# Retention woven into the attention in small steps, modulation sums by column groups, and a down projection that turns its tiles later

## The chip, the cores and the metric

One core of a Trainium2 chip. The metric is the device time of one execution in microseconds (us). TensorE (PE) multiplies a stationary 128-row tile with a moving one, VectorE (DVE), ScalarE (ACT) and GpSimd (POOL) work elementwise, SyncE (SP) issues most DMAs. Each engine runs its instructions in program order.

## The reference

Two layers of a trunk of width 1024 over 9 tiles of 128 tokens: 8 latent tiles and one context tile (`CTX` = 8). All in float32.

```
each layer:  h = rmsnorm(x) * g1 * (1 + scale) + shift        # modulation: six rows of 1024 per layer,
             q,k,v.. = h @ w_in                                #   silu(c) @ w_ada + b_ada, for c and c_ctx
             A = retention(q, k, v)     B = Fourier mixing
             C = latent attention       D = long convolution   # 4 x 256 columns
             x = x + gate * rmsnorm([A B C D] @ w_out) * g2
             x = x + gate * rmsnorm(swiglu(h2) @ w_down) * g4

retention, per head (4 of 64), forward and backward over chunks of 128 tokens:
   S[j+1] = gamma^128 * S[j] + (k * zeta)^T v
   o[j]   = (q k^T * D) v  +  (q * xi) S[j]
```

The final retention states of the context are an output too.

## The kernel before

The layers run one after the other, each in stages: input projection with convolution ("phase 1"), Fourier, retention and attention ("phase 2"), output projection ("phase 3"), the gate and up products of the FFN (`gate_up`, a Strassen scheme, 22 hidden blocks), and the down projection (`ffn`). The source lists instructions with priorities; a scheduler turns them into one fixed order per engine, with semaphores between engines.

**Modulation** (`ada_steps`, from L254). The two conditioning rows are multiplied with the 6144 columns of `wada` in groups of 256 columns: eight loads `adw` of 128x256 (L263); for row 0 VectorE adds each, scaled, into `adacc0` (L160, called by L267); for row 1 ScalarE scales it into `adp` (L272) and GpSimd adds (L157). TensorE then sums over the 128 partitions, with the 128x2 selector `sel` as the stationary tile: two products with `adacc0` and `adacc1` into `psada`, 2x256 (L285). VectorE adds the bias (`r`, in an `adw` buffer, loaded by L280) and multiplies by the norm's gain (`ng`, in an `adp` buffer, L282), and a DMA stores the row (L290). `adw` and `adp` have two buffers, `adacc` one. The function is a generator, advanced between products: the last 16 groups of layer 0 run in its phase 1 (there VectorE does both rows), the 24 of layer 1 in layer 0's `gate_up`, five advances for each group.

**Retention** (`ret_rope`, `ret_tables`, `ret_states`, `ret_tile`, `ret_group`). `ret_states` makes the nine (k * zeta)^T v (`pskv`, L1062), copies their diagonal blocks into `Sall` (L1071) and runs the recurrence on VectorE. All of that stands ahead of the attention, with a higher priority. `ret_tile` then makes one tile: four turns (L1088), four score products on 64 rows (L1100), the decay (L1101), and for each head one product with `v` (L1107) and two with the states, of 64 rows and 64 columns (L1110).

**Attention** (`attention`, L946). 20 items (a head and a pair of tiles) in a pipeline: scores of item n (L129 to L131, each product as three of split operands), turns of n - 1 (L918, L923), values of n - 2 (L935, L936, L938, result `o` L942). After the values it calls `beside(n)`, which advances the retention by one tile or group: 20 calls, 12 of them with work.

**Down projection** (`ffn`, from L1469). Three groups of three tiles; the products `dq` of a group go over 22 hidden blocks, in seven runs per tile. After the last run of a tile `finish` follows: norm of the product, `y` (L160), `x + y` (L157, on GpSimd for tiles up to `ET`, which is tile 7 in layer 0 and 1 in layer 1), then in layer 0 the norm and modulation of the next layer (L313, and the shift on the same engine as `x + y`), and at once eight turns (`norm_turn`, L324) whose results are the next layer's input.

Of the kernel before, what the change touches and what calls it, by code (L numbers as in the profile page):

```python
# [99 lines left out]
class Kern:  # L100
# [137 lines left out]
    def load_cond(self):  # L238
# [6 lines left out]
        self.sel = self.cp.tile([P, 2, 2], F32, name="sel")  # L245
        nc.vector.memset(self.sel, 0.0)
        for i in range(2):
            nc.vector.memset(self.sel[:, i, i:i + 1], 1.0)
# [5 lines left out]
    def ada_steps(self, l, c0, n, pool, psp, tag, dve=(0, 1)):  # L254


        nc, A = self.nc, self.A
        for c in range(c0, 6 * D, n):
            s, hs = c // D, slice(c % D, c % D + n)
            acc = [pool.tile([P, n], F32, name=f"adacc{i}", bufs=1) for i in range(2)]  # L260
            for kt in range(8):
                w = pool.tile([P, n], F32, name="adw", bufs=2)
                nc.sync.dma_start(w, A["wada"][l, kt, :, c:c + n])  # L263
                for i in range(2):
                    cs = self.cs[:, kt, i:i + 1]
                    if i in dve and kt:
                        self.stt(acc[i], w, cs, acc[i], ALU.mult, ALU.add)  # L267
                    elif i in dve:
                        self.ts("v", acc[i], w, cs)
                    else:  # L270
                        d = acc[i] if kt == 0 else pool.tile([P, n], F32, name="adp", bufs=2)
# [6 lines left out]
            k = {1: 0, 2: 1, 4: 2, 5: 3}.get(s)  # L278
            r, ng = (pool.tile([P, n], F32, name=nm, bufs=2)[:2] for nm in ("adw", "adw" if len(dve) > 1 else "adp"))
            nc.sync.dma_start(r, A["bada"][l, s:s + 1, hs].broadcast_to([2, n]))  # L280
            if k is not None:
                nc.sync.dma_start(ng, A["normg"][l, k:k + 1, hs].broadcast_to([2, n]))  # L282
            ps = psp.tile([2, n], F32, name="psada", tag=tag)
            for i in range(2):
                nc.tensor.matmul(ps, self.sel[:, i], acc[i], start=i == 0, stop=i == 1)  # L285
            nc.vector.tensor_tensor(out=r, in0=ps, in1=r, op=ALU.add)
            if k is not None:
                nc.vector.scalar_tensor_tensor(out=r, in0=r, scalar=1.0 if s in (1, 4) else 0.0, in1=ng,
                                               op0=ALU.add, op1=ALU.mult)
            nc.sync.dma_start(self.mods[l, s][:, hs], r)  # L290
            yield
# [654 lines left out]
    def attention(self, l, pool, hd, psp, beside):  # L946
# [6 lines left out]
        for n in range(len(pairs) + 2):  # L953
# [24 lines left out]
    def ret_tables(self, l, pool, Sall):  # L978
# [33 lines left out]
        scratch = Sall[:, 4:8].rearrange("p t a b c -> p (t a b c)").rearrange("p (n c) -> p n c", c=P)  # L1012
# [15 lines left out]
    def ret_rope(self, l, keep):  # L1028
# [4 lines left out]
        Sall = keep.tile([P, 8, 2, 2, 64], F32, name="Sall")  # L1033
        self.qk = keep.tile([P, NT, 512], F32, name="rqk")
        for t in range(NT):
            if t % 3 == 0:
                nc.sync.dma_start(self.qk[:, t:t + 3], self.proj[l][:, t:t + 3, 256:768])
            if t < CTX:
                tmp = Sall[:, 2 * (t % 2):2 * (t % 2) + 2].rearrange("p a b c d -> p (a b c) d")
# [3 lines left out]
    def ret_states(self, l, zt, gt, Sall, keep, psp):  # L1043

        nc, A = self.nc, self.A
        kvc = keep.tile([P, 2, 2, 64], F32, name="kvc")
        kzs = keep.tile([P, 2, 2, 4, 64], F32, name="rkz", tag="ropeR")
        for d in range(2):
            nc.sync.dma_start(Sall[:, 7 * d, :, d], A["sret"][l, :, :, d])
        for t in range(NT):  # L1050
            if t % 3 == 0:
                v3 = keep.tile([P, 3, 256], F32, name="rv")
# [11 lines left out]
            for hh in range(2):  # L1064
# [4 lines left out]
                for d, dst in ((0, t + 1), (1, t - 1)):  # L1069
                    if 0 <= dst < 8:  # L1070
                        nc.scalar.activation(Sall[q, dst, :, d], ps[q, :, d, q], AF.Copy)  # L1071

        nc.sync.dma_start(A["o_st"][l], kvc)
        for d, order in ((0, range(1, 8)), (1, range(6, -1, -1))):
            for t in order:
                prev = t - 1 if d == 0 else t + 1
                tmp = keep.tile([P, 2, 64], F32, name="rst")
                self.tt("v", tmp, Sall[:, prev, :, d], gt[:, :, d:d + 1].broadcast_to([P, 2, 64]), ALU.mult)
                self.tt("v", Sall[:, t, :, d], Sall[:, t, :, d], tmp, ALU.add)

    def ret_tile(self, l, t, vg, o, Dm, xi, Sall, pool, psp):
# [7 lines left out]
        qkT = pool.tile([P, 4, P], F32, name="rqkT")  # L1089
        nc.scalar.activation(qkT, ps, AF.Copy)  # L1090
        if lat:
            qx = pool.tile([P, 2, 2, P], F32, name="rqx")
            self.tt("g", qx, qkT[:, 0:2].unsqueeze(2).broadcast_to([P, 2, 2, P]), xi, ALU.mult)

# [7 lines left out]
        for e in range(2):  # L1102
            q = slice(64 * e, 64 * e + 64)
            pi = psp.tile([P, 2, 64], F32, name="psr", tag="r")
            for pr in range(2):
                h = 2 * pr + e
                nc.tensor.matmul(pi[:, pr], sT[:, h], vg[:, 64 * h:64 * h + 64], start=True, stop=not lat)  # L1107
                if lat:
                    for d in range(2):
                        nc.tensor.matmul(pi[:, pr], qx[q, pr, d], Sall[q, t, pr, d], start=False, stop=d == 1)  # L1110
            nc.scalar.activation(o[:, e::2], pi, AF.Copy)

    def ret_group(self, l, g, Dm, xi, Sall, pool, psp):

        nc = self.nc
        vg = pool.tile([P, 3, 512], F32, name="rvg")
        o = pool.tile([P, 12, 64], F32, name="ro", bufs=1)
        for j in range(3):
            self.ret_tile(l, 3 * g + j, vg[:, j], o[:, 4 * j:4 * j + 4], Dm, xi, Sall, pool, psp)
            yield  # L1120
# [19 lines left out]
        for j in range(3):  # L1140
# [3 lines left out]
            rt = pool.tile([P, 2, P], F32, name="rot", bufs=4)  # L1144
# [61 lines left out]
    def phase2(self, l):  # L1206
        nc, tc, A = self.nc, self.tc, self.A
        with ExitStack() as c:
# [478 lines left out]
```

## Time and profile before

| | us |
|---|---|
| median of 3 runs | 3466.37 (3465.84 to 3473.54) |
| the profiled execution | 3473.78 |
| its span | 3472.0 |
| PE busy | 3195.8 (92%) |
| DVE busy | 2421.7 (70%) |
| ACT busy | 1269.0 (37%) |
| POOL busy | 704.6 (20%) |

The stages, read from the timeline by their lines: layer 0 has phase 1 up to 560 us, phase 2 up to 848, phase 3 up to 965, `gate_up` up to 1537 and the down projection up to 1850; in layer 1 they end at 2240, 2551, 2660, 3178 and 3472. A busy PE is not a PE at full speed: PEclk is the share of its full clock that it was granted.

### The profile page before, as it was taken

The page shows a single profiled execution, that of the slowest core. Times are in us where ns is not written, and L with a number is a line of the kernel's source. Part 1 is how long each engine was busy: PE and PEld are TensorE (multiplying, and loading weights), DVE is VectorE, ACT ScalarE, POOL GpSimd, SP SyncE. Part 2 cuts the span into 40 slices and gives each one's busy share as a digit, 9 for nine tenths or more (in the row PEclk, how much of TensorE's full clock was granted, in tenths as well). Part 3 has the DMA queues.
Part 4 walks back from the last instruction along what each step waited for, and adds up shares of the span by engine and source line. Part 5 has one row for each costly group of instructions (what it writes and reads, how often), then busy time and mean ns, then how long its engine had stood idle before and what let it go on. Part 6 is the DMA issues. An engine that isn't in the chain of part 4 may idle for free.

```text
span 3472.0 us, 52651 instructions
## 1 busy us (share of the span) xinstructions
PE 3195.8 (92%) x19198; PEld 2844.6 (82%) x19198; DVE 2421.7 (70%) x4806; ACT 1269.0 (37%) x2384; POOL 704.6 (20%) x625
## 2 busy tenths in 40 slices
PE   8889888999969999989988999899997999998998
PEld 5768777888769999977777788798886899998887
DVE  6676887767898888874456637676688866665454
ACT  3123213555344444443333232254544322223332
POOL 2101110001244545521111011100112422220000
PEclk8799999889989999999999999998898999999999
DMA  5354555114333434364554444541053322225564
GB/s 213 102 173 141 156 166 179 39 38 138 104 124 118 124 114 123 103 204 163 174 170 138 136 125 142 172 125 34 23 172 110 94 77 77 77 65 172 173 206 142
DMA packets 343827, 444.64 MB, mean 128 GB/s; under 512 B 63338, under 2 KB 273511, under 8 KB 343056
## 3 DMA queue, kind: packets, MB, share of 16 engines
q1 hardware_dynamic: 281792, 384.31, 35.5%
q10 hardware_dynamic: 61776, 56.97, 5.4%
q8 instruction: 151, 2.47, 0.3%
q14 instruction: 108, 0.88, 0.1%
HBM read 349.17 MB, written 92.00 MB: 127 GB/s over the span
## 4 chain that ended last, share of the span: by engine, by line
PE 56%; DVE 21%; DMA 10%; issue 5%; ACT 4%; POOL 3%; SPq 0%; DVEq 0%; ACTq 0%; POOLq 0%
DMA adw<-in_wada 7%; PE gu L129 5%; PE gu L131 5%; PE gu L130 5%; PE dq L129 4%; PE dq L131 4%; PE dq L130 4%; DVE adacc L160 3%; PE acc L131 3%; PE acc L130 2%; PE acc L129 2%; PE pstr L918 1%; PE psr L1110 1%; DVE rq_w L146 1%; DVE fw L125 1%
## 5 line engine op out<-in xcount | busy, mean ns | idle before, releaser
L129 PE MATMUL dq<-dw 128*128 128x512 f32 x792 | 312.4, 394 | 13.5 <-ACT dw L120 10.8
L130 PE MATMUL dq<-dw 128*128 128x512 f32 x792 | 312.4, 394 | 0.0
L131 PE MATMUL dq<-dw 128*128 128x512 f32 x792 | 311.3, 394 | 0.0
L129 PE MATMUL gu<-X,fw 128*128 128x256 f32 x1024 | 286.8, 283 | 7.7 <-ACT fw L120 4.2
L160 DVE SCALAR_TENSOR_TENSOR adacc<-adw,csilu,adacc 128x256 f32<-128x256 f32 x392 | 228.5, 609 | 86.2 <-DMA adw<-in_wada 84.8
L131 PE MATMUL gu<-X,fw 128*128 128x256 f32 x1024 | 284.3, 280 | 1.9 <-DVE fw L125 1.9
L130 PE MATMUL gu<-X,fw 128*128 128x256 f32 x1024 | 283.8, 280 | 0.0
L130 PE MATMUL acc<-wlo,Th 128*128 128x256 f32 (+1 forms) x720 | 214.0, 297 | 6.6 <-DVE wlo L125 6.6
L125 DVE TENSOR_TENSOR dw<-dhr,dw 128x384 fp32r<-128x384 f32 x132 | 74.4, 569 | 208.5 <-ACT dw L120 207.2
L129 PE MATMUL acc<-whi,Th 128*128 128x256 f32 (+1 forms) x720 | 215.8, 302 | 0.8 <-ACT whi L120 0.4
L131 PE MATMUL acc<-whi,Tl 128*128 128x256 f32 (+1 forms) x720 | 214.5, 298 | 0.0
L129 PEld LDWEIGHTS gu<-X,fw 128*128 128x128 f32 x1024 | 193.7, 190 | 18.6 <-ACT fw L120 7.0
L131 PEld LDWEIGHTS gu<-X,fw 128*128 128x128 f32 x1024 | 193.6, 190 | 2.3 <-DVE fw L125 2.3
L130 PEld LDWEIGHTS gu<-X,fw 128*128 128x128 f32 x1024 | 193.7, 190 | 0.0
L129 PEld LDWEIGHTS dq<-dw 128*128 128x128 f32 x792 | 151.1, 191 | 47.1 <-ACT dw L120 11.9
L157 POOL TENSOR_TENSOR adacc<-adacc,adp 128x256 f32<-128x256 f32 x168 | 151.8, 903 | 160.7 <-ACT adp L272 157.1
L125 DVE TENSOR_TENSOR dw<-dwr,dw 128x1024 fp32r<-128x1024 f32 x132 | 161.4, 1225 | 31.3 <-ACT dw L120 31.2
L129 PE MATMUL gu<-x1s,fw 128*128 128x320 f32 x576 | 179.3, 311 | 3.7 <-DVE u L157 3.1
L131 PE MATMUL gu<-x1s,fw 128*128 128x320 f32 x576 | 179.4, 312 | 1.9 <-DVE fw L125 1.7
L130 PE MATMUL gu<-x1s,fw 128*128 128x320 f32 x576 | 179.0, 311 | 0.0
L131 PEld LDWEIGHTS dq<-dw 128*128 128x128 f32 x792 | 151.0, 191 | 32.5 <-DVE dw L125 1.3
L130 PEld LDWEIGHTS dq<-dw 128*128 128x128 f32 x792 | 151.2, 191 | 31.2
(494 smaller groups left out, 9432.5 us busy)
## 6 DMA issues: line engine op xcount, KB each, us to landing
dwr<-in_wf SPq DMA_DIRECT2D x132, 512.0 KB
adw<-in_wada SPq DMA_DIRECT2D x320, 128.0 KB
dhr<-h SPq DMA_DIRECT2D x132, 192.0 KB
h<-U SPq DMA_DIRECT2D x176, 128.0 KB
X<-in_wf SPq DMA_DIRECT2D x42, 512.0 KB
fr<-in_wf SPq DMA_DIRECT2D x40, 512.0 KB
pj<-pst ACTq DMA_DIRECT2D x90, 128.0 KB
r<-mod SPq DMA_DIRECT2D x20, 512.0 KB
```

Of the source, the lines that this page charges most:

```text
L125: (nc.vector if elo == "dve" else nc.gpsimd).tensor_tensor(out=lo, in0=src, in1=hi, op=ALU.subtract)
L129: mm(ps, lh, rh, start=start, stop=False)
L130: mm(ps, lh, rl, start=False, stop=False)
L131: mm(ps, ll, rh, start=False, stop=stop)
L146: nc.vector.scalar_tensor_tensor(out=w, in0=a, scalar=a[:, 0:1], in1=v, op0=ALU.mult, op1=ALU.mult)
L157: (self.nc.vector if e == "v" else self.nc.gpsimd).tensor_tensor(out=out, in0=a, in1=b, op=op)
L160: self.nc.vector.scalar_tensor_tensor(out=out, in0=a, scalar=s, in1=b, op0=op0, op1=op1)
L918: T(pst[:, j], pr[i][:, (k0 + j) * P:(k0 + j + 1) * P], self.ident)
L1110: nc.tensor.matmul(pi[:, pr], qx[q, pr, d], Sall[q, t, pr, d], start=False, stop=d == 1)
```

## The change

1. **Sums of the modulation.** Per group, four products instead of two: 32 stationary columns of ones, 128 moving columns, each into its own 32 partitions of a 128x128 `psada`. Bias, gain and result move in two DMAs each. In `gate_up` the sum stands three advances later (`late=3`), `adacc` has two buffers, `adp` one (which `ng` shares), and a group takes four advances instead of five.
2. **Retention.** `ret_states` and a tile's three parts are advances of their own: 11 for the states, 27 for tiles, 6 for groups, 44 together. `beside(n)` is also called after each scores: 64 calls. A state in `Sall` is 128 columns wide with zeros off the diagonal, so the product with the states takes 128 rows and columns, four for a tile instead of eight, and one copy `ro` instead of two.
3. **Down projection.** `x + y` and the shift are VectorE's for all tiles. The turns wait in a list `late`; one entry is taken after the first run of the next group's first tile, or when there are two.

```diff
+        def total(c, acc):
...
+            r, ng = (pool.tile([P, n], F32, name=nm, bufs=1 if late and nm == "adp" else 2)[:, :m]
+                     for nm in ("adw", "adw" if len(dve) > 1 else "adp"))
...
+            for h in range(2):
+                for i in range(2):
+                    q = 64 * h + 32 * i
+                    nc.tensor.matmul(ps[q:q + 32], self.ones[:, 0:32], acc[i][:, m * h:m * h + m], start=True, stop=True,
+                                     tile_position=(0, q))
...
-            acc = [pool.tile([P, n], F32, name=f"adacc{i}", bufs=1) for i in range(2)]
+            acc = [pool.tile([P, n], F32, name=f"adacc{i}", bufs=2 if late else 1) for i in range(2)]
...
+                    step += 1
+                    if todo and todo[0][0] <= step:
+                        total(*todo.pop(0)[1:])
                     yield
+            step += 1
+            todo.append((step + late, c, acc))
+            if not late:
+                yield
+                total(*todo.pop(0)[1:])
             yield
...
                 if i < len(score):
                     probs[n].append(self.att_scores(score[i], ops[h], pool, psp))
+                beside(n)
...
-        Sall = keep.tile([P, 8, 2, 2, 64], F32, name="Sall")
+        Sall = keep.tile([P, 8, 2, 2, P], F32, name="Sall")
...
+        pi = psp.tile([P, 4, 64], F32, name="psr", tag="r")
+        for pr in range(2):
+            both = pi[:, 2 * pr:2 * pr + 2].rearrange("p h e -> p (h e)")
+            if lat:
+                nc.tensor.matmul(both, qx[:, pr, 0], Sall[:, t, pr, 0], start=True, stop=False)
+            for h in (2 * pr, 2 * pr + 1):
+                nc.tensor.matmul(pi[:, h], sT[:, h], vg[:, 64 * h:64 * h + 64], start=not lat, stop=not lat)
+            if lat:
+                nc.tensor.matmul(both, qx[:, pr, 1], Sall[:, t, pr, 1], start=False, stop=True)
+        nc.scalar.activation(o, pi, AF.Copy)
+        yield
...
-                zt, gt, Dm, xi = self.ret_tables(l, rk, Sall)
-                self.ret_states(l, zt, gt, Sall, rk, psp)
+                tabs = self.ret_tables(l, rk, Sall)
...
+            steps = self.retention(l, tabs, Sall, rk, rp, psp)
...
-                ada = self.ada_steps(1, 0, 256, adp, banks, "ad", (0,))
+                ada = self.ada_steps(1, 0, 256, adp, banks, "ad", (0,), 3)
...
-                    self.tt(e, x[:, q], x[:, q], y[:, q], ALU.add)
+                    self.tt("v", x[:, q], x[:, q], y[:, q], ALU.add)
...
-                    self.norm_mod(t, x, y, rows[1], rows[2], dn, "tr", None, e)
+                    self.norm_mod(t, x, y, rows[1], rows[2], None, None, None, "v")
+                    late.append((t, y))
...
+                        if len(late) > 1 or late and f0 == 3:
+                            self.norm_turn(*late.pop(0), dn, "tr")
                         if f0 + n == NF:
                             finish(3 * g + j, ps[j])
```

What the scheduler makes of it, at three places. First TensorE's order in the attention of layer 0, around one retention tile. Before (`sc` scores, `pstr` turns, `psr` the retention's products, `psr<-Sall` those with the states):

```order
L918 MATMUL pstr<-ident,pr 128x128 x4
L1100 MATMUL psr<-rqkT 128x128 x4
L918 MATMUL pstr<-ident,pr 128x128 x2
L1107 MATMUL psr<-rvg,rsT 128x64
L1110 MATMUL psr<-Sall,rqx 128x64 x2
L1107 MATMUL psr<-rvg,rsT 128x64
L1110 MATMUL psr<-Sall,rqx 128x64 x2
L918 MATMUL pstr<-ident,pr 128x128 x3
```

And after the change:

```order
L131 MATMUL sc<-at_Tl_5835,at_Th_5834 128x384
L1142 MATMUL psr<-Sall,rqx 128x128
L1144 MATMUL psr<-rvg,rsT 128x64 x2
L1146 MATMUL psr<-Sall,rqx 128x128
L1142 MATMUL psr<-Sall,rqx 128x128
L1144 MATMUL psr<-rvg,rsT 128x64 x2
L1146 MATMUL psr<-Sall,rqx 128x128
L937 MATMUL pstr<-ident,pr 128x128 x8
```

A tile's products with the states are four instead of eight, and scores stand between them and the tile's turns and scores, which have moved to other items.

Second TensorE's order in `gate_up` of layer 0, around one sum of the modulation (`gu` are the products of the stage). Before:

```order
L130 MATMUL gu<-x1s_9234,fw 128x320
L131 MATMUL gu<-x1s_9233,fw 128x320
L285 MATMUL psada<-adacc_12001,sel 2x256
L285 MATMUL psada<-adacc_12002,sel 2x256
L129 MATMUL gu<-X_8153,fw 128x256
L130 MATMUL gu<-X_8154,fw 128x256
```

After:

```order
L129 MATMUL gu<-x1a_9249,fw 128x320
L272 MATMUL psada<-adacc_11481,ones 32x128
L130 MATMUL gu<-x1a_9250,fw 128x320
L272 MATMUL psada<-adacc_11482,ones 32x128
L272 MATMUL psada<-adacc_11481,ones 32x128
L272 MATMUL psada<-adacc_11482,ones 32x128
L131 MATMUL gu<-x1a_9249,fw 128x320
```

A sum is four products, here split by one of the stage's own. Counted over the whole stage in units of one hidden block (168 products `gu`), the 24 sums stand from 2.86 to 22.0, 0.83 apart, before, and from 3.29 to 20.32, 0.74 apart, after.

Third VectorE's order at the end of tile 0 of layer 0's down projection (the small operations between are those of the square root). Before:

```order
L160 SCALAR_TENSOR_TENSOR y_16753<-dq,rs,r_16537 128x1024
L303 TENSOR_SCALAR ss<-ss 128x1
...
L125 TENSOR_TENSOR dw<-dhr,dw 128x384
L313 SCALAR_TENSOR_TENSOR y_16753<-x_16543,rs,r_16539 128x1024
L150 SCALAR_TENSOR_TENSOR rq_u<-rq_w,rs 128x1
L125 TENSOR_TENSOR dw<-dwr,dw 128x1024
```

After:

```order
L160 SCALAR_TENSOR_TENSOR y_16877<-dq,rs,r_16661 128x1024
L157 TENSOR_TENSOR x_16667<-x_16667,y_16877 128x1024
L322 TENSOR_SCALAR ss<-ss 128x1
...
L125 TENSOR_TENSOR dw<-dhr,dw 128x384
L332 SCALAR_TENSOR_TENSOR y_16877<-x_16667,rs,r_16663 128x1024
L150 SCALAR_TENSOR_TENSOR rq_u<-rq_w,rs 128x1
L125 TENSOR_TENSOR dw<-dwr,dw 128x1024
L157 TENSOR_TENSOR y_16877<-y_16877,r_16665 128x1024
```

Both adds are now VectorE's. In TensorE's order the turns of the three tiles of a group stand 55, 84 and 112 products `dq` behind the tile's last one, before 47, 76 and 94.

## Rows read from the trace of the kernel before

**Rows 1.** Windows by stage: from:to, length, busy time of PE, PEld, DVE, ACT, POOL with instructions, PEclk, DMA share, GB/s.

```profile
594.00:848.00 254.00, 232.72 (x1462) 208.68 (x1462) 179.80 (x526) 140.32 (x301) 19.04 (x14) 0.89 0.23 67
1050.00:1500.00 450.00, 439.61 (x3206) 416.63 (x3205) 386.35 (x676) 190.67 (x376) 232.65 (x226) 1.00 0.39 115
1545.00:1850.00 305.00, 282.54 (x1225) 232.60 (x1224) 153.35 (x280) 106.07 (x161) 39.59 (x15) 0.96 0.52 169
2290.00:2551.00 261.00, 247.04 (x1621) 225.30 (x1621) 178.30 (x513) 142.43 (x303) 19.03 (x14) 0.90 0.23 68
2750.00:3150.00 400.00, 400.00 (x3067) 400.00 (x3066) 246.71 (x458) 116.68 (x200) 94.87 (x73) 1.00 0.24 70
3195.00:3472.00 277.00, 265.56 (x1170) 218.98 (x1168) 131.36 (x218) 91.41 (x134) 5.71 (x2) 0.99 0.54 179
```

**Rows 2.** Groups by line, 594 to 848 us, PE: count, busy us, mean ns, idle before.

```profile
L1110 PE MATMUL psr<-Sall,rqx 64*128 64x64 f32 x128 | 23.5, 306 | 0.0
```

**Rows 3.** Timeline of PE in layer 0's attention: start, length, line, count; end of a tile.

```profile
671.40 0.43 PE L1107 MATMUL psr<-rvg,rsT 128*128 128x64 f32 x2
671.76 0.66 PE L1110 MATMUL psr<-Sall,rqx 64*128 64x64 f32 x4
672.35 0.43 PE L1107 MATMUL psr<-rvg,rsT 128*128 128x64 f32 x2
...
673.97 1.11 PE L1110 MATMUL psr<-Sall,rqx 64*128 64x64 f32 x4
675.02 0.69 PE L129 MATMUL sc<-at_Tl,at_Th 96*128 96x384 f32 x1
```

**Rows 4.** Timeline of PE: six products of the states, in layer 1.

```profile
2312.45 0.83 PE L1062 MATMUL pskv<-rv,rkz 128*128 128x128 f32 x6
2313.04 0.42 PE L129 MATMUL sc<-at_Tl,at_Th 96*128 96x384 f32 x1
```

**Rows 5.** Chain of waits, 600 to 616 us.

```profile
602.94 6.26 DMA rv<-pj
```

**Rows 6.** The sums of `gate_up` (950 to 1545 us): all (minimum/median/maximum ns, first and last start), then two in the timeline.

```profile
L285 PE MATMUL psada<-adacc,sel x96: 377/378/634, 1059.1 to 1537.2; 128*2 128x256 f32 x96
...
1119.25 1.07 PE L285 MATMUL psada<-adacc,sel 128*2 128x256 f32 x4
...
1535.97 1.86 PE L285 MATMUL psada<-adacc,sel 128*2 128x256 f32 x4 [12.21 <-DVE adacc L160]
```

**Rows 7.** VectorE's scaled adds, 1050 to 1500 us: the idle before them, and what ended it.

```profile
L160 DVE SCALAR_TENSOR_TENSOR adacc<-adw,csilu,adacc 128x256 f32<-128x256 f32 x152 | 115.7, 761 | 36.0 <-DMA adw<-in_wada 35.1
```

**Rows 8.** One sum's buffer `adp` with the gain: its load on SP, and the last reader on DVE.

```profile
1381.86 0.25 SPq L282 DMA_DIRECT2D adp<-in_normg  x1
...
1389.76 0.41 DVE L288 SCALAR_TENSOR_TENSOR adw<-adw,adp 2x256 f32<-2x256 f32 x1
```

**Rows 9.** Waits of PE for the sums in phase 1 (0 to 560 us), total, times, longest.

```profile
PE psada L285 <- DVE adacc L160: 10.8, 7, 4.4
```

**Rows 10.** Waits of PE in layer 0's down projection (1545 to 1850 us).

```profile
PE pstr L324 <- POOL y L157: 21.7, 7, 4.6
```

**Rows 11.** Timeline, end of tile 0 in layer 0's down projection.

```profile
1622.83 2.39 POOL L157 TENSOR_TENSOR x<-x,y 128x1024 f32<-128x1024 f32 x1 [87.99 <-DVE y L160]
1630.13 3.27 POOL L157 TENSOR_TENSOR y<-y,r 128x1024 f32<-128x1024 f32 x1 [4.91 <-issue]
1628.33 0.39 PE L129 MATMUL dq<-dw 128*128 128x512 f32 x1
1628.56 0.39 PE L130 MATMUL dq<-dw 128*128 128x512 f32 x1
1633.46 1.97 PE L324 MATMUL pstr<-ident,y 128*128 128x128 f32 x8 [4.52 <-POOL y L157]
1636.51 0.63 PE L131 MATMUL dq<-dw 128*128 128x512 f32 x1
```

**Rows 12.** Groups by line: VectorE's add of a tile.

```profile
L157 DVE TENSOR_TENSOR x<-x,y 128x1024 f32<-128x1024 f32 (+1 forms) x28 | 33.0, 1184 | 0.8
```

More of the change, by code (lines that the diff above doesn't have):

```diff
@@ L252, in load_cond, with ada_steps @@
         self.mods = {(l, s): self.dram([2, D], f"mod{l}_{s}") for l in range(L) for s in range(6)}
[L254 removed]
+    def ada_steps(self, l, c0, n, pool, psp, tag, dve=(0, 1), late=0):
         nc, A = self.nc, self.A
+        m = n // 2
+        def total(c, acc):
+            s, hs = c // D, slice(c % D, c % D + n)
+            k = {1: 0, 2: 1, 4: 2, 5: 3}.get(s)
+            r, ng = (pool.tile([P, n], F32, name=nm, bufs=1 if late and nm == "adp" else 2)[:, :m]
+                     for nm in ("adw", "adw" if len(dve) > 1 else "adp"))
+            half = [slice(hs.start + m * h, hs.start + m * h + m) for h in range(2)]
+            for h in range(2):
+                nc.sync.dma_start(r[64 * h:64 * h + 64], A["bada"][l, s:s + 1, half[h]].broadcast_to([64, m]))
+                if k is not None:
+                    nc.sync.dma_start(ng[64 * h:64 * h + 64], A["normg"][l, k:k + 1, half[h]].broadcast_to([64, m]))
+            ps = psp.tile([P, m], F32, name="psada", tag=tag)
+            for h in range(2):
+                for i in range(2):
+                    q = 64 * h + 32 * i
+                    nc.tensor.matmul(ps[q:q + 32], self.ones[:, 0:32], acc[i][:, m * h:m * h + m], start=True, stop=True,
+                                     tile_position=(0, q))
+            nc.vector.tensor_tensor(out=r, in0=ps, in1=r, op=ALU.add)
+            if k is not None:
+                nc.vector.scalar_tensor_tensor(out=r, in0=r, scalar=1.0 if s in (1, 4) else 0.0, in1=ng,
+                                               op0=ALU.add, op1=ALU.mult)
+            for h in range(2):
+                nc.sync.dma_start(self.mods[l, s][:, half[h]], r[64 * h:64 * h + 64:32])
+        step, todo = 0, []
         for c in range(c0, 6 * D, n):
[L259 to L260 removed]
+            acc = [pool.tile([P, n], F32, name=f"adacc{i}", bufs=2 if late else 1) for i in range(2)]
             for kt in range(8):
@@ L270, in ada_steps @@
                     else:
-                        d = acc[i] if kt == 0 else pool.tile([P, n], F32, name="adp", bufs=2)
+                        d = acc[i] if kt == 0 else pool.tile([P, n], F32, name="adp", bufs=1 if late else 2)
                         nc.scalar.activation(d, w, AF.Copy, scale=cs)
@@ L275, in ada_steps @@
                 if kt == 3 or len(dve) < 2 and kt in (1, 5):
+                    step += 1
+                    if todo and todo[0][0] <= step:
+                        total(*todo.pop(0)[1:])
                     yield
-            yield
[L278 to L291, printed above, removed]
+            step += 1
[3 more added lines that the diff above has]
+                total(*todo.pop(0)[1:])
+            yield
+        for x in todo:
+            total(*x[1:])
     def row(self, dst, l, s, t):
@@ L1076, in ret_states, with retention @@
                 prev = t - 1 if d == 0 else t + 1
-                tmp = keep.tile([P, 2, 64], F32, name="rst")
-                self.tt("v", tmp, Sall[:, prev, :, d], gt[:, :, d:d + 1].broadcast_to([P, 2, 64]), ALU.mult)
-                self.tt("v", Sall[:, t, :, d], Sall[:, t, :, d], tmp, ALU.add)
+                for k in range(2):
+                    self.stt(Sall[:, t, k, d], Sall[:, prev, k, d], gt[:, k, d:d + 1], Sall[:, t, k, d], ALU.mult, ALU.add)
+            yield
+    def retention(self, l, tabs, Sall, keep, pool, psp):
+        zt, gt, Dm, xi = tabs
+        yield from self.ret_states(l, zt, gt, Sall, keep, pool, psp)
+        for g in range(3):
+            yield from self.ret_group(l, g, Dm, xi, Sall, pool, psp)
     def ret_tile(self, l, t, vg, o, Dm, xi, Sall, pool, psp):
@@ L1101, in ret_tile @@
             nc.vector.tensor_tensor(out=sT[:, e::2], in0=pe[e], in1=Dm[:, e::2], op=ALU.mult)
[L1102 to L1111, printed above, removed]
+        yield
+        pi = psp.tile([P, 4, 64], F32, name="psr", tag="r")
[8 more added lines that the diff above has]
+        nc.scalar.activation(o, pi, AF.Copy)
+        yield
     def ret_group(self, l, g, Dm, xi, Sall, pool, psp):
         nc = self.nc
-        vg = pool.tile([P, 3, 512], F32, name="rvg")
+        vg = pool.tile([P, 3, 512], F32, name="rvg", tag="rvg")
         o = pool.tile([P, 12, 64], F32, name="ro", bufs=1)
         for j in range(3):
-            self.ret_tile(l, 3 * g + j, vg[:, j], o[:, 4 * j:4 * j + 4], Dm, xi, Sall, pool, psp)
-            yield
+            yield from self.ret_tile(l, 3 * g + j, vg[:, j], o[:, 4 * j:4 * j + 4], Dm, xi, Sall, pool, psp)
         st = self.sm.tile([P, 12], F32, name="rmu")
@@ L1466 @@
     RING, AH = 6, 3
-    ET = (7, 1)
     def ffn(self, l):
@@ L1558, in ffn @@
                             load_x(t)
+            for x in late:
+                self.norm_turn(*x, dn, "tr")
     def run(self):
```

30 lines of the change are left out of this document (15 added, 15 removed).

## The prediction

> **What bounds the kernel now.** The table comes first: TensorE is busy 92% of the span and no other engine above 70%, so the time is TensorE's work, its waits and the clock it is granted. The windows by stage [rows 1] say which of the three counts where. In layer 1's gate and up products TensorE is busy 400 of 400 us at a clock of 1.00, and layer 1's down projection has 0.99: nothing is to be had there. The attention of both layers has a clock of 0.89 and 0.90, with VectorE at 71% and 68%. Layer 0's down projection has 0.96 and 22 us of idle TensorE. Layer 0's gate and up products have a full clock and yet only 3206 matmul rows in 450 us, of which 88 (22 groups of four) are sums: 6.93 of the stage's own per us, against 3067 in 400, or 7.67, in layer 1 without a modulation. These three stages are what the change touches, and I went into each with the groups by line, the timeline and the waits.
>
> In the attention the reader is to see that the clock falls at the retention's products. Four rows with the states take 0.59 us (671.76 to 672.35), and a little later, in the same tile, 1.05 us (673.97 to 675.02) [rows 3]: the second are at the half clock, and the scores that follow run at it too. In the down projection it falls behind a wait: TensorE waits 4.52 us for GpSimd's add, and the `dq` behind it last 0.63 us instead of 0.39 [rows 11].
>
> **Retention.** The products with the states are 128 rows a layer [rows 2], and become 64: half as many, 128 rows high and 128 columns wide. Before, one costs 0.148 us at the full clock (0.59 / 4) and 0.26 at the half [rows 3]. For the new shape the nearest rows are the six products `pskv`, 128 by 128, in 0.59 us, or 0.098 each [rows 4]. So 128 x 0.148 - 64 x 0.098 = 12.7 us a layer at the full clock; I take **13**. More is possible: the 72 rows with `v` (nine tiles of eight) cost 0.18 each today (two from 671.40 to 671.76 [rows 3]) and would gain 6 if they fell to 0.098 too.
>
> The clock: 0.89 of 254 us means 56 us at half speed, which cost 28; layer 1's 0.90 of 261 cost 26 [rows 1]. A tile's last products are now 24 rows, 4 x (0.36 + 0.59) = 3.8 us at the full clock and nearly in one go; they become 16, at 0.098 some 1.6 us, with scores between them and the tile's other parts. Turns and head loads stay as they are, so I give back a third, **9 us** a layer, between 0 and 20. At the start of layer 0 the chain stands 6.26 us in a load of `rv` that the states wait for [rows 5]. As steps beside scores, TensorE has other work there: **6 us**, between 0 and 7. The states' other work (recurrence, copies) moves beside the attention too. If this cover failed, VectorE would be next: 180 busy us of 254 become 180 of some 229, or 79%, so it holds. A copy of `ro` less and a GpSimd fill of zeros lie on engines at 55% and 7%: nothing. Phase 2: 2 x (13 + 9) + 6 = **50 us**, between 25 (2 x 12.7) and 85 (2 x (13 + 6 + 20) + 7).
>
> **Down projection, layer 0.** Its seven waits for GpSimd's shift are 21.7 us [rows 10]. The clock costs 0.04 x 305 = 12 us, against 0.01 x 277 = 3 in layer 1, which has no turns [rows 1]: 9 hang on the waits, so 31 are at stake. Tile 0 shows how much of it goes. GpSimd's two adds take 2.39 and 3.27 us [rows 11]; VectorE's take 1.18 each [rows 12]: 3.3 us earlier. The turns stand 8 products later, at 0.23 each (1628.33 to 1628.56 [rows 11]) 1.8 us. Together 5.1 against a wait of 4.52: it just goes, and it goes with more room where the distance grew by 18. The adds cost VectorE 16 x 1.18 = 19 us more in a stage in which it is busy 153 of 305 [rows 1]: hidden, though they stand in front of the splits `dw`, which TensorE needs some blocks later. I leave 5 us of waits at the first tiles of groups: **26 us**, between 18 and 33. What is late next is the same chain, through the square and the root on ScalarE and VectorE.
>
> **Modulation in gate_up.** The 24 sums run from 1059.1 to 1537.2 us; the last waits 12.2 us [rows 6] at the end of the stage, where I count 11 as the turn to the next stage. That leaves 467 / 23 = 20.3 us a group. TensorE's own part: 0.83 of a hidden block of 168 products, at layer 1's 7.67 per us 21.9 us a block, plus 1.07 for the sum at 1119.25 [rows 6], 19.2. So 1.1 us a group is lost to the stream that feeds the sum. Part of it is the loads: VectorE idles 35 us for `adw` in 450 [rows 7].
>
> After, a group is 0.74 of a block: TensorE's own part is 17.3 us. The stage then needs 23 periods, and 0.43 blocks more ahead and 1.68 behind: 23 p + 46 us, against 467 now. That is **equal at p = 18.3**; at 17.3 it saves 23; if the stream stays at 20.3, TensorE waits for it at each sum, and 46 are lost. The late sum and the second pair of accumulators let the next group begin without the sum; against it stands the single `adp`. Two SP issues more per sum are 0.25 us each [rows 8], on a queue with room. I leave 0.8 of the 1.1 us: p = 18.1, **5 us** saved, between 23 saved and 46 lost.
>
> The four products of a sum move 128 columns each, not 256, and there are twice as many; I price them as the old pair, 1 us. From the retention's rows the bounds are 0.25 (all four at once) and 1.6 (a change of shape dearer by the 0.16 us that a pair with `v` takes over two `pskv`, up to four times where a sum is split): for 24 groups 18 us less to 14 more.
>
> Against this form speaks the Trainium skill, "TensorEngine Tiling (Array Packing)", section "Key Properties": "Changing tiling mode (not just tile) drains the TensorE", while different tiles may run in parallel. No row of the kernel before has a 32-column product, but the mixed heights of the retention agree with a drain (0.18 us for 64 columns beside 0.098 for 128). By the drain alone the 40 sums of both layers would cost some 20 us more (two to four changes of 0.16 each) and the time be near 3405; by four tiles in parallel 30 less (0.75 each) and near 3355; my sum goes between them.
>
> **Phase 1** of layer 0 takes the new sums without the delay: 10.8 us of waits for VectorE [rows 9] stay, since VectorE's adds are the same. 0, between 8 less and 8 more.
>
> **Sum.** 50 + 26 + 5 = 81 us. Durations come from the execution of 3473.8 us (span 3472.0), 7 above the median of the three runs; it would become 3393, and I take the 81 off the median: 3466.4 - 81 = **3385**.
>
> **Rivals.**
> 1. *The clock stays low.* The products of the states shrink, but turns and head loads keep the half clock, and the first load is only moved. For it: half of the tile's rows are still short products. Phase 2 then saves 26: 3409. Chance 0.17.
> 2. *The stream cannot run denser.* For it: VectorE waits for `adw` today and is busy 386 of 450 us; the sums in the new order stand right behind their last add. Against: the drained accumulators are gone. Then 46 are lost instead of 5 won: 3436. Chance 0.17.
> 3. *The single `adp` stalls the stream: slower.* Gain and partial product now share one buffer. In one sum of before, the gain held its buffer from 1381.86 to 1390.17, 8.3 us [rows 8]. If ScalarE stands still so long for each of the 16 groups that have a gain, GpSimd, the accumulators and TensorE's next sum wait with it: 16 x 8.3 = 133 us, 3518. It decides from 81 / 23 = 3.5 us a group above 18.1, a period of 21.6. Against it: the late sum has its inputs ready, so the hold shrinks to a load and two short operations. Chance 0.09.
> 4. *More comes back.* The clock and the rows with `v` recover (phase 2 at 75) and no wait is left at the sums: 3338. Chance 0.07. Here belongs also that the change does less than it says: in the order the sums do not stand later than their last add, so "late" may buy nothing; that is rival 2.
>
> **How the numbers follow.** My own case has the remaining 0.5, from 3355 to 3412 by its bounds. About 0.3% (10 us) is what a measurement can tell from no change. Cases 1, 2 and 4 and my own are faster, less a few hundredths at the end of rival 2: faster 0.87, same 0.05, slower 0.08. The range 3340 to 3440 leaves out rival 3 and the best part of 4.
>
> **What would show it.** In the attention, a clock of 0.92 to 0.94, 64 rows with the states at about 0.1 us, 229 and 239 us between the same lines. In the down projection, waits for the turns below 6 us and a clock of 0.98. In `gate_up`, the distance of sums near 18.1 us; above 21.6 the forecast is wrong in sign. A clock still at 0.89 would put rival 1 in its place.

## The result, and the profile after

The changed kernel takes 3504.4 us (median, 3496.9 to 3508.0) against 3470.0 before (3465.8 to 3475.3): a ratio of 1.0089, with a 95% interval of 1.0067 to 1.0112. It is **slower**, by 0.9%, where 3385 and faster was forecast.

The stages, each from its first product to the first one of the next in the profiled executions:

| stage | forecast | before | after | difference |
|---|---|---|---|---|
| layer 0, phases 1 and 2 | -28 | 838.0 | 835.7 | -2.3 |
| layer 0, gate and up | -5 | 572.7 | 631.8 | +59.1 |
| layer 0, down projection | -26 | 311.0 | 282.1 | -28.9 |
| layer 1, phases 1 and 2 | -22 | 692.5 | 694.8 | +2.3 |
| all others | 0 | | | below 4 |

So the down projection came as forecast, the retention's 50 us came to nothing, and the modulation went far to the other side. Neither miss alone turned the sign: the differences add up to some 30 us, and with either the modulation or the retention as forecast the kernel would still have been faster, by 20 to 35 us. The windows by stage after (columns as in [rows 1]): the attention of layer 0, its gate and up, its down projection, and the attention of layer 1.

```profile
601.90:835.70 233.80, 205.82 (x1375) 184.34 (x1373) 189.13 (x575) 139.69 (x296) 24.64 (x16) 0.91 0.28 84
1100.00:1500.00 400.00, 352.78 (x2527) 336.87 (x2526) 297.08 (x544) 158.01 (x308) 198.13 (x191) 0.94 0.39 114
1600.00:1876.00 276.00, 273.83 (x1230) 225.08 (x1229) 155.51 (x290) 106.08 (x161) 0.00 (x0) 1.00 0.58 186
2347.30:2570.80 223.50, 192.26 (x1326) 175.86 (x1324) 185.18 (x563) 133.23 (x278) 22.93 (x16) 0.91 0.26 78
```

The down projection has a clock of 1.00 instead of 0.96, and TensorE idles 2 us in 276. Gate and up had full clock and 439.6 busy us in 450; now TensorE is idle 47 us of 400, at 0.94. VectorE there fell from 86% to 74%: its own work is not what holds things up. The sums of the stage (as in [rows 6]):

```profile
L272 PE MATMUL psada<-adacc,ones x192: 269/297/423, 1066.0 to 1545.0; 128*32 128x128 f32 x192
```

And its waits (900 to 1600 us; total, times, longest):

```profile
ACT adp L295 <- DMA adw<-in_wada: 96.6, 57, 5.1
...
ACT adp L295 <- POOL adacc L157: 55.0, 56, 2.9
...
PE psada L272 <- DVE adacc L160: 46.1, 20, 4.9
...
ACT adp L295 <- DVE adw L276: 33.7, 12, 5.4
```

24 sums from 1066.0 to 1545.0 are 20.8 us a group, not 18.1, and TensorE waits at 20 of them (46.1 us, 2.3 each; before 19.2, of which 12.2 was the last). The prediction's own formula, 23 p + 46 against 467, gives 524, or 57 lost.

In the attention the products with the states have halved as planned; the mean row with `v` fell from 300 to 272 ns (groups by line, 594 to 848 us; [rows 2]):

```profile
L1144 PE MATMUL psr<-rvg,rsT 128*128 128x64 f32 x72 | 11.2, 272 | 0.0
...
L1146 PE MATMUL psr<-Sall,rqx 128*128 128x128 f32 x32 | 7.6, 323 | 0.0
L1142 PE MATMUL psr<-Sall,rqx 128*128 128x128 f32 x32 | 7.0, 302 | 0.2 <-PE pstr L937 0.2
```

What took the gain back is to be seen in layer 1. TensorE waits once, 14.7 us, for VectorE; VectorE rotates the retention's queries and keys in one piece from 2355.92 on; and these wait for their tables and rows, whose loads SP issues only at 2349.78, behind phase 1's last staging buffer (the last store of it at 2347.95). The waits of PE, 2340 to 2376 us:

```profile
PE pstr L937 <- DVE rt L1011: 14.7, 1, 14.7
```

And the timelines of ACT, SP and DVE there:

```profile
2347.95 0.33 ACTq L753 DMA_DIRECT2D pj<-pst  x1
...
2349.78 0.33 SPq L1052 DMA_DIRECT2D ropeR<-in_ropeR  x1
2350.16 1.49 SPq L1057 DMA_DIRECT2D rqk<-pj  x3
...
2355.92 1.09 DVE L157 TENSOR_TENSOR Sall<-rqk,ropeR 128x256 f32<-128x256 f32 x3
...
2370.46 0.68 DVE L157 TENSOR_TENSOR rqk<-rqk,Sall 128x512 f32<-128x512 f32 x1
```

Before, the same load stood at 2246.30, 67 us ahead of the attention's start (2313.0), beside phase 1's products:

```profile
2246.30 0.33 SPq L1032 DMA_DIRECT2D ropeR<-in_ropeR  x1
```

In the two programs' allocation the retention's pool `rk` starts at byte 128032 of each partition before and at 125952 after, because `rot` gave up two of four buffers; phase 1's staging buffers end at 127008 and 126976. The first tile of the pool, `ropeR`, now lies over their last KB.

### The profile page after: what moved, and what is told of

It is laid out like the page before. It is cut to its first block, busy times and chain, and to the rows that moved or that the text cites. A ratio compares the mean times of both kernels' runs of the same rounds, so it can differ in the third digit from the quotient of the medians.

```text
span 3498.8 us, 52737 instructions
## 1 busy us (share of the span) xinstructions
PE 3171.8 (91%) x19230; PEld 2834.1 (81%) x19230; DVE 2398.9 (69%) x4821; ACT 1272.8 (36%) x2366; POOL 659.2 (19%) x611
## 4 chain that ended last, share of the span: by engine, by line
PE 56%; DVE 20%; DMA 10%; issue 5%; ACT 4%; POOL 3%; SPq 1%; DVEq 0%; ACTq 0%; POOLq 0%
PE gu L131 5%; PE gu L130 5%; PE gu L129 5%; DMA adw<-in_wada 5%; PE dq L129 4%; PE dq L131 4%; PE dq L130 4%; PE acc L130 3%; PE acc L131 3%; PE acc L129 3%; DVE adacc L160 2%; POOL adacc L157 2%; DVE rq_w L146 1%; PE pstr L937 1%; DVE fw L125 1%
## 5 line engine op out<-in xcount | busy, mean ns | idle before, releaser
L129 PE MATMUL dq<-dw 128*128 128x512 f32 x792 | 310.4, 392 | 21.7 <-ACT dw L120 21.2
L131 PE MATMUL dq<-dw 128*128 128x512 f32 x792 | 309.7, 391 | 0.0
L160 DVE SCALAR_TENSOR_TENSOR adacc<-adw,csilu,adacc 128x256 f32<-128x256 f32 x392 | 220.2, 587 | 75.6 <-DMA adw<-in_wada 74.7
L129 PEld LDWEIGHTS dq<-dw 128*128 128x128 f32 x792 | 149.9, 189 | 54.6 <-ACT dw L120 21.7
L129 PE MATMUL gu<-x1s,fw 128*128 128x320 f32 x576 | 183.5, 319 | 6.0 <-DVE u L157 3.1
L131 PE MATMUL gu<-x1s,fw 128*128 128x320 f32 x576 | 183.0, 318 | 1.9 <-DVE fw L125 1.8
L130 PE MATMUL gu<-x1s,fw 128*128 128x320 f32 x576 | 182.8, 317 | 0.1
```

Of the source, the lines that this page charges most:

```text
L129: mm(ps, lh, rh, start=start, stop=False)
L130: mm(ps, lh, rl, start=False, stop=False)
L131: mm(ps, ll, rh, start=False, stop=stop)
L160: self.nc.vector.scalar_tensor_tensor(out=out, in0=a, scalar=s, in1=b, op0=op0, op1=op1)
```

## The experiments

Each time is a median, each ratio against the kernel before, with its interval. The kernel before, run again beside each group of experiments, had medians of 3467.4 to 3471.9 us. The same instructions also vary between profiles: layer 0's phases 1 and 2 took 838.0 us before and 829.0 in experiment 1, which does not touch them. So some 5 us between two experiments, or 9 in that stage, are not to be read as an effect.

**1. The down projection alone** (kernel before with the changed `ffn`).

> The kernel before with the change's down projection alone. If the 29 us that this stage lost between the two profiles (311.0 to 282.0 us from its first product to the next stage's first) is the work of the VectorE adds and the later turns alone: 27 to 31 us faster than before, near 3441. If part of it came from what the other parts of the change do to memory or to the clock: less than 20.

3439.6 us, 0.9910 (0.9881 to 0.9938); the stage 281.5 us. The term stands by itself.

**2. The old modulation** (changed kernel; `ada_steps`, its selector and its call as before).

> The changed kernel with the modulation of before (selector sums at once, two adp buffers, five advances a group). If the stream of the modulation alone makes the gate and up stage 59 us longer: 55 to 65 faster than the changed kernel, near 3443, and this stage back at 573 us. If the wider states or the deferred turns share in it by where they put the buffers: the stage stays above 600 and the time above 3470.

3425.0 us, 0.9869 (0.9840 to 0.9897): 79 less than the changed kernel, more than the 55 to 65 expected. The stage is back at 571.0. Most of the rest is layer 0's phases 1 and 2, 821.8 instead of 835.7. Only 4 of these 14 us lie ahead of the attention's first scores (598.3 instead of 601.9); the others lie behind them, where 48 of Fourier's 84 products stand with the new sums and 12 with the old.

**3. The retention's buffers moved up.** A pad makes `rk` start at 126976, where the staging buffers end; six small tables make room for it.

```diff
+                rp.tile([P, 160], F32, name="rpad", bufs=1)
-                tabs = self.ret_tables(l, rk, Sall)
+                tabs = self.ret_tables(l, rk, rp, Sall)
...
-        x = pool.tile([P, 8], F32, name="rdec")
+        x = rp.tile([P, 8], F32, name="rdec")
```

> The changed kernel with 1 KB more per partition ahead of the retention's buffers (a pad of 640 bytes and six small tables moved there), so that the rotary table no longer lies over the last KB of phase 1's staging buffers. If this overlap is what holds the retention's loads until phase 1 has ended: the loads start some 70 us earlier in layer 1, VectorE's 14 us of rotation leave the attention, and each layer's phase 2 is 12 to 25 us shorter, in all 3455 to 3480. If the late start comes from weaving itself: within 6 us of the changed kernel.

3471.0 us, 1.0011 (0.9993 to 1.0029): 33 less (27 by the ratios). The load stands at 2263.88, 64 us ahead of the attention's start at 2327.7:

```profile
2263.88 0.33 SPq L1052 DMA_DIRECT2D ropeR<-in_ropeR  x1
```

The clock of the attention in layer 1 goes from 0.91 to 0.95 (window):

```profile
2327.70:2534.00 206.30, 188.79 (x1326) 172.33 (x1324) 169.63 (x531) 132.99 (x278) 22.92 (x16) 0.95 0.22 68
```

Not one operation was added or taken away. Layer 1's phases 1 and 2 fall from 694.8 to 671.0, layer 0's from 835.7 to 827.2.

**4. The gain out of `adp`** (the gain's row in the unused half of the bias buffer).

```diff
-            r, ng = (pool.tile([P, n], F32, name=nm, bufs=1 if late and nm == "adp" else 2)[:, :m]
-                     for nm in ("adw", "adw" if len(dve) > 1 else "adp"))
+            r = pool.tile([P, n], F32, name="adw", bufs=2)
+            r, ng = r[:, :m], r[:, m:]
```

> The changed kernel with the gain's row in the unused half of the bias buffer instead of the single adp. If ScalarE's waits behind the gain (33.7 us, 12 times) are what stretches the groups: 25 to 40 us faster than the changed kernel. If the single adp's taking turns between ScalarE and GpSimd (53.9 us of waits, 55 times) or the denser order sets the pace: under 12 us faster.

3495.3 us, 1.0079 (1.0052 to 1.0106): 9 less, and none of it in the stage, which is 639.4. The 33.7 us behind the gain were real waits, and cost nothing: ScalarE then waited for `adw` instead, 132 us where it was 90 (1050 to 1590 us). So the gain's hold on `adp`, the mechanism of the prediction's third rival, is not what stretches the groups. The edit also touches phase 1, where the gain held an `adw` buffer: the last sum there stands at 532.1 us instead of 567.0, and phases 1 and 2 of layer 0 take 828.8 instead of 835.7.

**5. Five advances instead of four** for a group, all else as changed.

> The changed kernel with five advances a group instead of four; late sum, two accumulator pairs and the single adp stay. If the stream has a pace of its own near 20.3 to 20.8 us a group and TensorE only waits because its order expects 17.3: the gate and up stage (631.8 us in the changed kernel) comes back to 570 to 590 and the time to 3445 to 3465. If the single adp makes the stream slower than before at any plan: the stage stays above 605.

3469.1 us, 1.0005 (0.9991 to 1.0020). The stage is 600.1: between the two bands. The pace hardly changed (1066.6 to 1559.3, less 11 for the turn at the end, 20.9 a group), but TensorE's order now fits it and the clock is 1.00 through most of the stage: half of the loss is gone. So half of it was the order's haste. Of the 27 us that stay, 10 are also there in experiment 7, with the old timing. The others belong to the late sum, the second accumulators and the single `adp` together, which were not tried one by one. In the trace TensorE now waits for VectorE's results of the stage's own products (1050 to 1580 us), for which it never waits in that stretch of the kernel before:

```profile
PE gu L129 <- DVE u L157: 14.4, 15, 2.2
PE gu L129 <- DVE G L157: 7.2, 10, 1.5
```

**6. A third `adw` buffer** (with the gain as in 4, `adp` still single; room from a narrower `ones` and two `sm` buffers for three).

> The changed kernel with a third adw buffer and the gain beside the bias in it; adp stays single. Room for it comes from a narrower constant of ones and two instead of three buffers for the small sums. If the bias row, which holds one of two adw buffers for some 10 us of each group, keeps the loads from running ahead: groups 18 to 19 us apart, the stage 570 to 600, the time 3445 to 3475. If the single adp sets the pace: above 615, the time within 15 us of the changed kernel.

3463.3 us, 0.9982 (0.9962 to 1.0001). The groups are 17.1 us apart, about what the prediction had as TensorE's own part (17.3), and no sum stands among TensorE's waits any more. The single `adp` does not set the pace; the loads do. That they cannot run ahead because the bias holds one of two buffers fits this, but a third buffer was added and not the bias taken out, so it is the likely reading and not shown by itself. The sums:

```profile
L272 PE MATMUL psada<-adacc,ones x192: 272/285/298, 1058.8 to 1451.8; 128*32 128x128 f32 x192
```

The longest waits of PE from 1000 to 1560 us, and a window of the stage:

```profile
PE gu L129 <- DVE G L157: 15.5, 26, 1.0
PE gu L129 <- DVE u L157: 13.2, 17, 2.9
```

```profile
1100.00:1450.00 350.00, 324.05 (x2386) 302.49 (x2386) 296.00 (x523) 151.16 (x302) 187.99 (x193) 0.99 0.44 128
```

And yet the stage is 591.6, where the formula (23 x 17.1 + 46 against 467) gives 545: TensorE now waits for VectorE's evictions of the stage's own products (28.7 us), with VectorE at 85%. Up to 8 us are this edit's own: layer 1's gate and up, which has no modulation, is 515.3 instead of 507.3.

**7. Column sums alone** (old timing and buffers, the four 32-column products stay).

> The changed kernel with the sums at once, five advances and two adp buffers as before: of the modulation's change only the four 32-column products remain. If their form costs about what the old pair did (0.6 to 1.3 us a group): the stage 565 to 580, the time 3420 to 3440, as with the old sums. If the change of shape drains TensorE at its price of up to 0.65 us more: 15 us above that.

3451.5 us, 0.9958 (0.9940 to 0.9976); the stage 582.7. The time lies in the second band (3435 to 3455), 12 us above the first, but by waits and not by the products: from the product ahead of each sum to the one behind it, the 24 sums take 59.6 us (54.5 before), and from a sum's first product to the next other one 21.7 (28.8 before): the products are cheaper, the waits 12 us longer. A sum that waits for nothing shows the price of the form itself; here one of this run with its neighbours, then one of the kernel before:

```profile
1053.24 0.31 PE L131 MATMUL gu<-x1a,fw 128*128 128x320 f32 x1
1053.47 0.43 PE L272 MATMUL psada<-adacc,ones 128*32 128x128 f32 x8
1053.83 0.38 PE L129 MATMUL gu<-X,fw 128*128 128x256 f32 x1
```

```profile
1098.96 0.31 PE L131 MATMUL gu<-x1s,fw 128*128 128x320 f32 x1
1099.20 1.02 PE L285 MATMUL psada<-adacc,sel 128*2 128x256 f32 x4
1100.15 0.39 PE L129 MATMUL gu<-X,fw 128*128 128x256 f32 x1
```

Both start 0.24 us behind the product ahead of them; the next product follows after 0.36 us, before after 0.95.

**8. Old modulation and moved buffers together**, with the changed retention and down projection.

> The modulation of before, the woven retention with its buffers moved as in memory_pad, and the changed down projection. If the two repairs are independent (79 us for the old sums, 33 for the memory): 3392 to 3405, faster than both kernels. If the old sums already gave back part of what the memory costs: 3410 to 3425.

3390.1 us, 0.9774 (0.9754 to 0.9793). The two repairs add up. Against the down projection alone (3439.6) the retention's part is worth 50 us (47 by the ratios), once its buffers don't collide.

**9. A third `adw` with the old modulation** (on 8).

> The kernel of old_sums_pad with a third adw buffer in the gate and up stage. If what TensorE still loses at the sums there (some 1.1 us a group) is the loads that cannot run ahead: the waits before the sums fall below 8 us in all and the stage from 572 to 555 to 565, the time 3375 to 3385. If VectorE, busy 85% of that stage, is the limit: the stage within 6 us, 3385 to 3395.

3393.8 us, 0.9784 (0.9765 to 0.9802), the stage 572.1: no gain. With the old order TensorE and VectorE (85%) are the limit, not the loads.

**10. The states ahead of the attention again** (on 8).

```diff
+                for _ in self.ret_states(l, tabs[0], tabs[1], Sall, rk, rp, psp):
+                    pass
...
-        yield from self.ret_states(l, zt, gt, Sall, keep, pool, psp)
```

> The kernel of old_sums_pad with the retention's states ahead of the attention again, as before; tiles stay in three steps and with the wide product. If weaving the states itself gives something (the load of rv and the short products beside scores): 8 to 20 slower than old_sums_pad, 3398 to 3410. If the gain of phase 2 is the wide products and the smaller tile steps alone: within 6 us of 3390.

3370.8 us, 0.9709 (0.9694 to 0.9723): 19 **less**, outside both bands. Weaving the states costs. This and the kernel of experiment 12 are the fastest. The states' products do not move ahead of the attention in time: in both kernels they start 15.4 us behind layer 0's first scores and 22.4 behind layer 1's. Woven, layer 0's last they until 635.4 us, 49 behind the first scores, here until 620.5, 32 behind (first and last start; woven, then here):

```profile
L1068 PE MATMUL pskv<-rv,rkz x72: 270/275/532, 601.9 to 635.4; 128*128 128x128 f32 x72
L1068 PE MATMUL pskv<-rv,rkz x72: 272/275/532, 603.8 to 620.5; 128*128 128x128 f32 x72
```

What moves is the tiles. Their results `ro` run, counted from the first scores, from 69 to 171 us woven and from 44 to 134 here in layer 0:

```profile
L1128 ACT ACTIVATE ro<-psr x9: 381/383/387, 655.9 to 757.4; 128x256 f32<-128x256 f32 x9
L1127 ACT ACTIVATE ro<-psr x9: 361/383/387, 632.6 to 722.6; 128x256 f32<-128x256 f32 x9
```

The states' 11 advances take calls of `beside` that the tiles could have had. Why that costs 19 us was not pursued further. The attention of both layers, first woven (8), with clocks of 0.93 and 0.96, then here, with 0.97 and 0.99:

```profile
586.40:802.70 216.30, 193.12 (x1346) 176.47 (x1344) 174.44 (x535) 137.43 (x287) 24.43 (x16) 0.93 0.25 74
2249.40:2454.40 205.00, 187.91 (x1326) 170.76 (x1324) 169.43 (x531) 132.84 (x278) 22.95 (x16) 0.96 0.23 68
```

```profile
588.30:789.10 200.80, 184.20 (x1308) 165.22 (x1308) 168.58 (x528) 134.17 (x279) 23.51 (x16) 0.97 0.26 79
2238.40:2431.00 192.60, 179.38 (x1290) 160.65 (x1289) 165.34 (x524) 128.44 (x269) 24.93 (x16) 0.99 0.24 72
```

And one tile's products with the states and with `v`, in layer 1; the `po` product is the next that is not the retention's:

```profile
2289.39 0.39 PE L1122 MATMUL psr<-Sall,rqx 128*128 128x128 f32 x2
2289.61 0.56 PE L1124 MATMUL psr<-rvg,rsT 128*128 128x64 f32 x4
2290.00 0.44 PE L1126 MATMUL psr<-Sall,rqx 128*128 128x128 f32 x2
...
2291.17 0.39 PE L938 MATMUL po<-ident,mx 128*128 128x128 f32 x2
```

**11. Later turns without VectorE's adds** (on 8).

> The kernel of old_sums_pad with both adds of the down projection on GpSimd again for the tiles where they were; the turns stay deferred. By the prediction's own sum for tile 0 (3.3 us from VectorE, 1.8 from the deferral, of a wait of 4.5) most of the waits come back: 8 to 18 us slower, the stage 290 to 300 instead of 280. If the deferral alone covers GpSimd's adds: within 4 us.

3421.0 us, 0.9856 (0.9840 to 0.9872): 31 slower, more than the 8 to 18 expected; the stage is 309.7. The whole gain is gone, and the waits are nearly the old ones. All eight of them, with the one behind the window of [rows 10], first before (1490 to 1880 us), then here (1490 to 1840 us):

```profile
PE pstr L324 <- POOL y L157: 23.3, 8, 4.6
```

```profile
PE pstr L324 <- POOL y L157: 21.7, 8, 4.3
```

**12. VectorE's adds without later turns** (on 10).

> The kernel of states_ahead with the turns of the down projection at once again; both adds stay on VectorE. If the adds carry the whole gain of that stage (turns_later_only lost all of it): the stage 280 to 284 us and the time within 5 us of 3371. If the deferral's 1.8 us at tile 0 is needed as the prediction has it (3.3 won of a wait of 4.5): waits of 1 us at each of some seven tiles and a little clock, the stage 287 to 296, 6 to 15 us slower.

3371.2 us, 0.9704 (0.9680 to 0.9728): nothing lost, the stage 280.5. The waits for the turns (1490 to 1840 us), of which the first lies behind the stage's end, at the last tile's turns:

```profile
PE pstr L324 <- DVE rs L150: 3.9, 1, 3.9
...
PE pstr L324 <- DVE y L157: 1.8, 5, 0.7
```

In TensorE's stream tile 0's turns stand behind 395 products before, 396 with the deferral alone, 403 with the adds alone and 403 with both. So at this tile the engine of the adds decides where the scheduler puts the turns. At the other two of the group the list even puts them earlier: behind 456 and 508 products with both, 461 and 523 with the adds alone, 448 and 490 before.

**13. Whole tiles** (on 10: a retention tile in one step, steps only after the values; the wide product stays).

> The kernel of states_ahead with a retention tile in one step again, and steps only after the values of an item, as before; the wide product stays. If the wide product carries what phase 2 gained (49 us of layer 0, 31 of layer 1 against before): within 6 us of 3371. If the small steps carry it, by the clock: 10 to 30 us slower.

3387.1 us, 0.9756 (0.9742 to 0.9771): 16 slower. In layer 1 the attention (first scores to the output projection) is 228.3 us before, 207.0 with the wide product in whole tiles, 192.6 with small steps too. So the steps are worth 14 there, and the wide product, with the buffers and VectorE's operations that changed beside it, 21. Part of the steps' gain goes back in phase 3, which is 142.2 us with small steps, 135.7 here and 140.3 before: together with it the two are worth 8 and 26 in layer 1, and the steps 7 in layer 0, which adds up to the 16. The clock of the attention is 0.89 in both layers before; here first layer 1 before, then this run with 0.95 and 0.97:

```profile
2313.00:2541.40 228.40, 214.44 (x1384) 194.00 (x1382) 166.08 (x488) 130.04 (x272) 19.03 (x14) 0.89 0.19 56
```

```profile
595.30:811.40 216.10, 192.98 (x1369) 172.13 (x1367) 175.92 (x540) 138.19 (x289) 22.61 (x16) 0.95 0.25 74
2259.20:2466.30 207.10, 188.12 (x1350) 170.06 (x1348) 171.69 (x536) 133.82 (x280) 22.65 (x16) 0.97 0.23 68
```

## Why the prediction was wrong, step by step

- **Modulation in `gate_up`: the largest failed step.** "I leave 0.8 of the 1.1 us: p = 18.1" took the period from TensorE's side. It was 20.8, slower even than before. The formula around it held (57 forecast by it, 59 measured), and so did rival 2 in its mechanism, which had the period at 20.3 and the loss at 46 us. What was missing was that the pace belongs to the loads: waits for the two `adw` buffers stand as `DMA adw` in [rows 7] and in ScalarE's waits. With a third buffer the period fell to 17.1 (6), and then VectorE's evictions held TensorE up. None of the kernels tried had a denser stream without such a cost.
- **The price of waiting.** With waits of 2.3 us at 20 of 24 sums TensorE's clock in the stage was 0.94 instead of 1.00; with a calmer order (5) it was 1.00 in most of it. The prediction counted the waits and not this.
- **The single `adp`** (rival 3): its waits are in the trace as the rival said, 55.0 and 33.7 us. Removing one (4) gained nothing in the stage, and with a third `adw` buffer (6) the other did not keep the period from 17.1.
- **The sums' form**: 21.7 us for 24 sums against 28.8 (7). "I price them as the old pair" was on the dear side. The drain that the Trainium skill ("TensorEngine Tiling (Array Packing)", "Key Properties") states for a change of tiling mode shows no price here: the sums of 32 columns start as soon behind a product of 128 as the old ones, 0.24 us, and are over sooner (7). The 12 us of experiment 7 are waits; why the same adds come later there was not tried.
- **Phase 1** was put at "0, between 8 less and 8 more": layer 0's phases 1 and 2 are 14 us longer with the new sums than with the old (2), and 24 with the buffers moved (3 against 8). That is outside the bounds, though the same instructions vary by up to 9, and part of it falls into phase 2, since Fourier's products move behind the scores. The last sum of phase 1 stands at 567.0 us instead of 539.5, and at 532.1 with the gain beside the bias (4); the cause was not pursued further.
- **Retention: a sum met by luck, and a step left out.** 50 us were forecast and none came. The step that failed is "as steps beside scores ... 6 us": weaving the states costs 19 (10). And a step was missing altogether: the prediction did not look where the smaller buffers put the others. That alone was worth 33 us (3), and the new sums cost the same two phases 14 (2). Without both, the retention's part gives the 50 us (8), but not as forecast: without the woven states it is 69, where 44 were set beside the 6 for weaving, and the weaving takes 19 of them. The price of the products held: 16 rows of a tile take 1.8 us in experiment 10, from 2289.39 to 2291.17, where 1.6 was forecast and 3.8 was the time before [rows 3]. The clock was undersized: "I give back a third". In the changed kernel it was 0.91 in both layers, below the 0.92 to 0.94 named as the sign; with the products wide, the states ahead and the tile in small steps (10) it came back almost wholly, to 0.97 and 0.99, and the turns and head loads that were to keep it low did not.
- **Down projection: right in size, wrong in its parts.** 26 forecast, 29 measured, the clock 1.00 for 0.98 expected. But the eight products' distance, 1.8 of the 5.1 us, was credited to the deferral; at tile 0 it comes with VectorE's adds (11, 12), which do all of the stage's gain.
- **The sums of the prediction** come out, but for two slips that decide nothing: 254 less 28 us is 226 and not 229 for layer 0's phase 2, and rival 4's two terms (25 and 18 us) lead to 3342 and not 3338. The range was too narrow for its own bounds: the worst ends of its terms, with the sums' 14 and phase 1's 8, add up to 3491, where the result is 3504.

## What to carry to other kernels

Before making a stream denser, find what sets its pace: here the adds waited for loads into two buffers, the new order did not make them faster, and TensorE, which runs its instructions in order, waited for them, with a lower clock as well. When buffers shrink or grow, look at what the others now lie over; here one load behind a late reader cost some 30 of the 50 us that were to be saved. Of a change in three parts measure the parts: here the best kernels (3370.8 and 3371.2 us) keep the wide product, the small tile steps and VectorE's adds, move the buffers, and take back the modulation and the woven states; the later turns make no difference to them.

## What was not expected of the hardware

TensorE's clock rose in the attention without TensorE idling less. In layer 1 it was 0.89 before, with 14 us of idle TensorE in 228; with the wide products and a tile still in one step 0.97, with 19 us in 207 (13); in small steps 0.99, with 13 us in 193 (10). So the idle time alone does not explain the clock. That half as many products, of 128 rows and columns instead of 64, do explain it is likely and not shown by itself: other operations and the buffers changed with them, the changed kernel has the same products at 0.91 with 31 us of idle TensorE in 223, and the attention of before reached 0.92 in layer 0 in experiment 1. A sum of four products of 32 stationary columns, each in its own partitions, took 0.36 us where nothing was waited for, against 0.95 for the two that it replaced.
